# Reordering one decoder-layer kernel: the last tile's eviction, the splits that open a block, and one unit of room in the attention chain

## The chip, the cores and the metric

The kernel runs on one core of a Trainium2 chip. The metric is the device time of one execution in microseconds (us). Before the change the median of three runs is 2895.75 us (2893.29 to 2896.04).

## What is computed

One step of a hybrid decoder layer in fp32, for a prompt of 2048 tokens and a sample group of 8 sequences with 4 tokens each, which share all weights. Cut to what matters:

```python
def hybrid_layer(x, ...):
    u, q, k, v, g_s, g_a = split(x @ w_in)                  # 512, 512, 128, 128, 1024, 1024 columns
    y, state = s5_scan(u, ...)                              # diagonal state space branch
    ya, yb = split(gelu(y) @ w_glu)
    branch_s = ya * sigmoid(yb)
    o = sliding_window_attention(q, k, v, sinks)            # window 128, 8 heads, 2 kv heads
    branch_a = o @ w_attn_br
    merged = sigmoid(g_s) * branch_s + sigmoid(g_a) * branch_a
    x = layer_norm(ALPHA * x + merged @ w_o)                # "x1"
    a, g = split(x @ w_up)                                  # 2 x 2816 columns
    h = gelu(causal_conv3(a)) * g
    return layer_norm(ALPHA * x + h @ w_down)
```

## The kernel before

**Precision.** Every matrix operand is cut into an upper part (fp32r) and a lower part (the rest), and a product is three matmuls: upper with upper, upper with lower, lower with upper. For a weight tile `wr` of 128 x 1024 (a *unit*), ScalarE (ACT in the profile) makes the upper part `wh` and VectorE (DVE) or GpSimd (POOL) the lower part `wl` by a subtraction. `Weights` (lines 181 to 219) does this ahead of the use: `load_to` issues the DMA on SyncE's queue (SP), `split_to(n, eng)` makes the two parts of all units up to `n`. Without `eng`, line 200 gives every third unit's lower part to POOL once 24 units are done; there are four buffers each for `wh` and `wl`, three for `wr`.

**Order.** Each engine's queue holds its instructions in the order in which the Python program issues them. The prompt is done in four blocks of 512 tokens (`body`), and the sample's 32 tokens ride along with block 1. A block goes through its units one after the other: `u` 0 to 3, `k`, `v`, four `q`, eight `gs` and eight `ga` gates (in block 0 the `q` come behind the `gs`), eight `glu`, four `br`, eight `wo`, then 22 pairs `ua`, `ug` and the `dn` units. 512 columns of one unit take TensorE (PE) some 5.5 us.

**Side work.** Between two units the program calls `bg.tick()` (`Background`, lines 48 to 76). Work that was added for this tick is issued then: first all that has no matmuls of its own, then the functions marked `@fills`, whose transposes and small matmuls go into TensorE's queue between two units; within each, what is further along its chain comes first. `ssm_chain` gives a chain of steps s0 to s9 for each quarter of the state space, `attn_chain` (lines 869 to 946) one for each of 4 query blocks x 2 kv heads: a0 scores (PE), a1 row maxima (DVE), a2 exponentials and sums (ACT, DVE), a3 the probabilities `pp` times the reciprocal sums `su` (POOL, 4 instructions), a4_ transposes of `pp` (PE) and their eviction `pt` (ACT), a6 the product with the values (PE), a7 its eviction to `oh` (ACT) and `ol` (DVE). One step is issued each tick. Chain i starts `AS*i//5` ticks behind the first, with 5 in block 0 (`AS0`), 7 in block 1 (`AS1`) and 9 in blocks 2 and 3 (`AS`). In block 0 the first starts at the tick behind the second `ga` unit, so that the last a7 is issued behind `glu` 6.

**Buffers.** PSUM tiles all come from `P()`, a pool of eight banks of 128 x 512; a tile is written only when the last reader of the bank's former tile is done. SBUF work tiles come from `S()`, a pool of 66.

**The stage around x1** (lines 1414 to 1559). The second half of `wo` is done token tile by token tile: `wo_second(t)` gives 24 matmuls, `wo_evict` adds the residual (`xr`, line 1431) and takes the statistics, `ln_scale` makes the reciprocal deviation on POOL (four small instructions, `rs`, lines 1143 to 1146), `ln1` applies it to the two halves of the row, one on ACT, one on DVE (line 1464). `x1_transpose(t)` brings the tile into PSUM by eight PE transposes, and `x1_evict(half)` turns two tiles into the operand of the next layer: `upper` writes the upper parts `x1h` of eight channel groups k, `whole` the exact values `x1f`, `lower` their differences `x1l`. For k below 4 these go through ACT, above through DVE. PE does `wo_second(3)` last, then `first_units` (line 1604): the upper products of the first two up-projection units over tiles 0 and 1, then those with `x1l`, then `x1_transpose(2)` and `x1_transpose(3)`, then unit three, which reads split +3. The order of DVE and POOL between these is written out by hand:

```python
        wo_evict(acc, 2, 1)
        ln_scale(2)
        upper()
        W.split_to(W.pos + 1, V)
        W.split_to(W.pos + 2, G)
        whole()
        ln1(2)
        lower(range(4))
        lower(range(4, 8), G)
        wo_evict(acc3, 3, 1)
        ln_scale(3)
        W.split_to(W.pos + 3, V)
        ln1(3)
        W.split_to(W.pos + 4, G)
```

**The sample's state** (`sample_state_out`, lines 1120 to 1127) is written out behind the last `glu` unit of block 1: for each of two parts a DVE copy `hso`, a PE transpose at once, an ACT eviction, a DMA on POOL's queue.

Of the kernel before, what the change touches and what calls it, by code (L numbers as in the profile page):

```python
# [8 lines left out]
F32 = mybir.dt.float32  # L9
# [3 lines left out]
OP = mybir.AluOpType  # L13
# [66 lines left out]
def tile_hybrid_layer(ctx: ExitStack, tc: tile.TileContext,  # L80
# [5 lines left out]
    V, A, G, T, SP = nc.vector, nc.scalar, nc.gpsimd, nc.tensor, nc.sync  # L86
# [15 lines left out]
    def S(name, cols=512, dt=F32):  # L102
        return pool.tile([128, cols], dt, name=uid(name), tag="s", bufs=SLOTS)
# [7 lines left out]
    def act(out, in_, func=AF.Identity, scale=1.0, bias=0.0, **kw):  # L111
        if func is AF.Identity and not isinstance(bias, bass.AP) and bias == 0.0 and not isinstance(scale, bass.AP):
            A.activation(out, in_, AF.Copy, scale=scale, **kw)  # L113
        else:
            A.activation(out, in_, func, scale=scale, bias=bias, **kw)  # L115
# [4 lines left out]
    def tt(out, a, b, op, eng=V):  # L120
        eng.tensor_tensor(out, a, b, op=op)  # L121
# [46 lines left out]
    order = []  # L168
# [12 lines left out]
    class Weights:  # L181
# [12 lines left out]
        def split_to(self, n, eng=None):  # L194
            while self.splits < min(n, len(order)):
                t = self.raw.pop(self.splits)
                hi = wp.tile([128, 1024], F32R, name=uid("wh"), tag="wh", bufs=4)
                lo = wp.tile([128, 1024], F32R, name=uid("wl"), tag="wl", bufs=4)
                act(hi, t)
                e = eng or (G if self.splits % 3 == 2 and self.splits > 24 else V)  # L200
                tt(lo, t, hi.bitcast(F32), OP.subtract, eng=e)
                self.ready[self.splits] = (hi, lo)
                self.splits += 1
# [17 lines left out]
    W = Weights()  # L221
    bg = Background()
# [60 lines left out]
    def transpose_to(out, in_, k):  # L283
        T.transpose(out, in_, ident[:k, :k])  # L284
# [584 lines left out]
    def attn_chain(B, qb, kv):  # L869
        C = Blk()  # L870
        first = B.b == 0 and qb == 0
        mk = mask[:, 2:4] if first else mask[:, 0:2]
        mk = mk.rearrange("p a k -> p (a k)")

        @fills
        def a0():
            C.s = [P(), P()]
            for j in range(4):
                o = C.s[j // 2][:, (j % 2) * 256:(j % 2) * 256 + 256]
                q = B.q[j][kv][:, qb * 128:(qb + 1) * 128]  # L880
                ks = slice(qb * 128, qb * 128 + 256)
                T.matmul(o, q, kh[kv][:, ks], start=True, stop=False)  # L882
                T.matmul(o, q, kl[kv][:, ks], start=False, stop=True)  # L883

        def a1():
            C.p = [S("pp"), S("pp")]
            C.nm = sm("nm", 4)
            for j in range(4):
                h = 4 * kv + j
                V.tensor_tensor_reduce(out=C.p[j // 2][:, (j % 2) * 256:(j % 2) * 256 + 256],  # L890
                                       in0=C.s[j // 2][:, (j % 2) * 256:(j % 2) * 256 + 256], in1=mk,
                                       scale=-0.125, scalar=nsk[:, h:h + 1], op0=OP.add, op1=OP.min,
                                       accum_out=C.nm[:, j:j + 1])
            C.es = sm("es", 4)
            tt(C.es, C.nm, sk[:, 4 * kv:4 * kv + 4], OP.add)

        def a2():
            C.sum = sm("su", 4)
            for j in range(4):
                o = C.p[j // 2][:, (j % 2) * 256:(j % 2) * 256 + 256]  # L900
                act(o, o, AF.Exp, scale=-1.0, bias=C.nm[:, j:j + 1], accum_out=C.sum[:, j:j + 1])
            act(C.es, C.es, AF.Exp)
            tt(C.sum, C.sum, C.es, OP.add)
            V.reciprocal(C.sum, C.sum)

        def a3():
            for j in range(4):
                o = C.p[j // 2][:, (j % 2) * 256:(j % 2) * 256 + 256]
                ts(o, o, C.sum[:, j:j + 1], eng=G)

        @fills
        def a4_():
            C.t = [P(), P()]
            for kt in range(2):
                for j in range(4):
                    o = (j % 2) * 256 + kt * 128
                    transpose_to(C.t[kt][:, j * 128:(j + 1) * 128], C.p[j // 2][:, o:o + 128], 128)

            B.pt[qb, kv] = [S("pt"), S("pt")]
            for kt in range(2):  # L920
                act(B.pt[qb, kv][kt], C.t[kt])
            C.__dict__.clear()

        @fills
        def a6():
            if kv == 1:
                B.ops[qb] = P()
                for h in range(2):
                    r = slice(64 * h, 64 * h + 64)
                    pt = B.pt.pop((qb, h))  # L930
                    for kt in range(2):
                        T.matmul(B.ops[qb][r, :], vt[:, qb + kt, r], pt[kt], start=(kt == 0), stop=(kt == 1))  # L932

        def a7():
            if kv == 1:
                ps = B.ops.pop(qb)
                sl = slice(qb * 128, (qb + 1) * 128)
                for j in range(4):
                    if j not in B.oh:
                        B.oh[j], B.ol[j] = S("oh", 544, F32R), S("ol", 544, F32R)  # L940
                    act(B.oh[j][:, sl], ps[:, j * 128:(j + 1) * 128])
                for j in range(4):
                    tt(B.ol[j][:, sl], ps[:, j * 128:(j + 1) * 128], B.oh[j][:, sl].bitcast(F32), OP.subtract)
                B.ready += 1

        return [a0, a1, a2, a3, a4_, a6, a7]


    def sample_consts(B):
# [168 lines left out]
        return [c0, None, c1, c2, c4, c6, c8]  # L1118

    def sample_state_out(B):  # L1120
        for r, dst in enumerate((re_s, im_s)):
            t = S("hso")
            V.tensor_copy(t[:, 0:128].rearrange("p (b a) -> p b a", b=8), B.hn[:, r].rearrange("p a b -> p b a"))
            ps = P()
            transpose_to(ps[:, 0:128], t[:, 0:128], 128)
            act(t[:, 128:256], ps[:, 0:128])
            G.dma_start(dst.rearrange("b (a g) p -> (b a) (g p)", g=2), t[:, 128:256])


    def ln_part(B, i, h):  # L1130
# [82 lines left out]
    def body(B, nxt):  # L1213
        n, cols = B.n, B.cols
# [4 lines left out]
        for i in range(4):  # L1219
            hi, lo = (w.rearrange("p (k m) -> p k m", k=2) for w in W.get(("u", i), 0 if B.b else max(0, 3 - i)))  # L1220
            for kk in range(2):
                k = 2 * i + kk
# [39 lines left out]
        ps = full(("k",))  # L1262
        for i, c0, c in segs:
            sl = slice(128 + c0, 128 + c0 + c)
# [3 lines left out]
            for h in range(2):  # L1268
                r = slice(64 * h, 64 * h + 64)
# [8 lines left out]
        ps = full(("v",))  # L1278
# [33 lines left out]
        if B.last:  # L1312
            t = S("kwo")
            ps = P()
# [141 lines left out]
        def ln_scale(i):  # L1456
            scales[i] = ln_stats(B, i)

        def ln1(i):
            m = rows(B, i)  # L1460
            rs = scales.pop(i)
            z = B.z[i]
            act(z[1][:m, 0:512], z[1][:m, 0:512], AF.Identity, scale=rs[:m, 0:1], bias=rs[:m, 1:2])
            ts(z[0][:m, 0:512], z[0][:m, 0:512], rs[:m, 0:1], rs[:m, 1:2], op0=OP.mult, op1=OP.add)
# [22 lines left out]
        def x1_evict(half):  # L1487
            def src(k):
                if half == 2:
                    return tps[4][:, k * 32:(k + 1) * 32]  # L1490
                return tps[half, k // 2][:, (k % 2) * 256:(k % 2) * 256 + 256]

            c0, c = (512, 32) if half == 2 else (half * 256, 256)
            sl = slice(c0, c0 + c)
            f = [S("x1f") for _ in range(4)]
            fk = lambda k: f[k // 2][:, (k % 2) * 256:(k % 2) * 256 + c]

            def affine(out, k):
                if k < 4 or half == 2:
                    act(out, src(k), AF.Identity, scale=g1[:, k:k + 1], bias=b1[:, k:k + 1])  # L1500
                else:
                    ts(out, src(k), g1[:, k:k + 1], b1[:, k:k + 1], op0=OP.mult, op1=OP.add)

            def upper():
                for k in (0, 4, 1, 5, 2, 6, 3, 7):
                    affine(x1h[k][:, sl], k)

            def whole():
                for k in (0, 4, 1, 5, 2, 6, 3, 7):
                    affine(fk(k), k)  # L1510

            def lower(ks=range(8), eng=V):
                for k in ks:
                    tt(x1l[k][:, sl], fk(k), x1h[k][:, sl].bitcast(F32), OP.subtract, eng)
            return upper, whole, lower

        def wo_second(t):
# [23 lines left out]
        ln_scale(2)  # L1541
        upper()
        W.split_to(W.pos + 1, V)
        W.split_to(W.pos + 2, G)
        whole()
        ln1(2)
        lower(range(4))
        lower(range(4, 8), G)
        wo_evict(acc3, 3, 1)
        ln_scale(3)  # L1550
        W.split_to(W.pos + 3, V)
        ln1(3)
        W.split_to(W.pos + 4, G)
        if B.sp:
            for fn in x1_evict(2):
                fn()
# [277 lines left out]
```

## Time and profile before

| | |
|---|---|
| median of 3 runs | 2895.75 us |
| the profiled execution | 2894.74 us |
| its span, first to last instruction | 2892.9 us |
| PE busy | 2833.0 us (98%) |
| PE weight loads | 2415.8 us (84%) |
| DVE, ACT, POOL busy | 59%, 40%, 36% |
| mean granted TensorE clock | 0.992 of 2.4 GHz |

PE is busy nearly all the time, so what can be won by reordering lies in the sixty microseconds in which it is not, and in the stretches in which its clock is granted at half. The share of the other engines says little: a wait ends with the one instruction that PE needs next, wherever that stands in its own engine's queue.

### The profile page before, as it was taken

What the parts mean: (1) busy time and instruction counts of PE and PEld (TensorE: products, weight loads), DVE (VectorE), ACT (ScalarE), POOL (GpSimd) and SP (SyncE); (2) the same over time, 40 slices, a digit from 0 to 9 for tenths busy, and PEclk for the clock granted to TensorE, in tenths of its full rate; (3) what the DMA queues carried; (4) which work ended last, traced back from release to release, by engine and by line L of the source; (5) the groups of instructions that cost most, each with busy time, mean ns of one, the idle gap of its engine ahead of it and who ended that gap; (6) DMA issues with size and microseconds to landing.
All of it is one profiled execution on the core that took longest, in us unless ns stands there. A gap on an engine that the chain in (4) does not pass through costs nothing. (4 is left out here: it accounts for less than half of the span.)

```text
span 2892.9 us, 39211 instructions
## 1 busy us (share of the span) xinstructions
PE 2833.0 (98%) x15168; PEld 2415.8 (84%) x15168; DVE 1696.7 (59%) x2678; ACT 1142.8 (40%) x1991; POOL 1047.3 (36%) x1098
## 2 busy tenths in 40 slices
PE   9989999999999999999999999999999999999998
PEld 8877888888998889989977778888888877888887
DVE  6985676254574467634646645673545854675355
ACT  3335354243335425423424352442343453354241
POOL 1964243111455313512216641351114652252122
PEclk9999999999999999999999999999999999999999
DMA  4422333234532232322326224233244523333232
GB/s 139 150 70 73 124 94 103 92 95 133 165 114 81 74 113 75 91 93 79 117 90 196 81 75 137 73 102 102 88 138 124 166 70 110 102 89 108 88 95 98
DMA packets 415116, 304.30 MB, mean 105 GB/s; under 512 B 52283, under 2 KB 351122, under 8 KB 414914
## 3 DMA queue, kind: packets, MB, share of 16 engines
q1 hardware_dynamic: 412114, 293.84, 33.3%
q0 software_dynamic: 2816, 7.96, 0.8%
q8 instruction: 119, 1.95, 0.3%
q14 instruction: 67, 0.55, 0.1%
HBM read 285.30 MB, written 17.39 MB: 105 GB/s over the span
## 5 line engine op out<-in xcount | busy, mean ns | idle before, releaser
L121 POOL TENSOR_TENSOR wl<-wr,wh 128x1024 fp32r<-128x1024 f32 x144 | 358.6, 2490 | 953.1 <-ACT wh L113 909.8
L113 ACT ACTIVATE wh<-wr 128x1024 fp32r<-128x1024 f32 x448 | 470.5, 1053 | 285.8 <-PE ps L239 187.6
L233 PE MATMUL ps<-x1l,wh 128*128 128x512 f32 (+2 forms) x1856 | 571.8, 343 | 2.0 <-DVE x1l L121 2.0
L233 PE MATMUL ps<-x1h,wh 128*128 128x512 f32 (+2 forms) x1856 | 569.4, 342 | 0.0
L233 PE MATMUL ps<-x1h,wl 128*128 128x512 f32 (+2 forms) x1856 | 568.9, 342 | 0.0
L121 DVE TENSOR_TENSOR wl<-wr,wh 128x1024 fp32r<-128x1024 f32 x304 | 395.5, 1304 | 219.8 <-ACT wh L113 219.2
L233 PEld LDWEIGHTS ps<-x1l,wh 128*128 128x128 f32 x1856 | 327.5, 189 | 45.1 <-DVE x1l L121 2.9
L233 PEld LDWEIGHTS ps<-x1h,wh 128*128 128x128 f32 x1856 | 327.0, 189 | 43.2
L233 PEld LDWEIGHTS ps<-x1h,wl 128*128 128x128 f32 x1856 | 326.4, 189 | 41.2
L233 PE MATMUL ps<-xh,wh 128*128 128x512 f32 (+1 forms) x880 | 288.0, 359 | 7.9 <-DVE q L121 2.5
L233 PE MATMUL ps<-xh,wl 128*128 128x512 f32 (+1 forms) x880 | 282.3, 354 | 1.5 <-DVE wl L121 1.5
L233 PE MATMUL ps<-xl,wh 128*128 128x512 f32 (+1 forms) x880 | 281.8, 353 | 0.0
L118 DVE SCALAR_TENSOR_TENSOR cv<-ae,pc,cv 128x512 f32<-128x512 f32 x176 | 145.6, 827 | 227.0 <-ACT cv L115 223.9
L237 PE MATMUL ps<-wh,hh 128*128 128x512 f32 x704 | 278.7, 396 | 0.0
L239 PE MATMUL ps<-wh,hl 128*128 128x512 f32 x704 | 277.8, 395 | 0.0
L238 PE MATMUL ps<-wl,hh 128*128 128x512 f32 x704 | 277.0, 393 | 0.0
L1571 POOL COPY cc<-ae 128x2 f32<-128x2 f32 x88 | 19.7, 223 | 472.2 <-ACT ae L113 471.3
L233 PEld LDWEIGHTS ps<-xh,wh 128*128 128x128 f32 x880 | 158.0, 191 | 31.8 <-issue 4.4
L233 PEld LDWEIGHTS ps<-xh,wl 128*128 128x128 f32 x880 | 157.4, 190 | 25.7 <-DVE wl L121 2.6
L233 PEld LDWEIGHTS ps<-xl,wh 128*128 128x128 f32 x880 | 157.9, 191 | 20.4
L125 POOL TENSOR_SCALAR pp<-pp,su 128x256 f32<-128x256 f32 x128 | 133.7, 1062 | 70.4 <-ACT pt L113 30.3
L237 PEld LDWEIGHTS ps<-wh,hh 128*128 128x128 f32 x704 | 132.8, 189 | 30.7
(363 smaller groups left out, 4956.9 us busy)
## 6 DMA issues: line engine op xcount, KB each, us to landing
wr<-in_w_up SPq DMA_DIRECT2D x176, 512.0 KB
wr<-in_w_in SPq DMA_DIRECT2D x88, 512.0 KB
wr<-in_w_down SPq DMA_DIRECT2D x88, 512.0 KB
wr<-in_w_glu SPq DMA_DIRECT2D x64, 256.0 KB
wr<-in_w_o SPq DMA_DIRECT2D x32, 512.0 KB
xin<-in_x_prompt SPq DMA_DIRECT2D x32, 256.0 KB
wr<-in_w_in SPq DMA_DIRECT2D x32, 256.0 KB
wr<-in_w_attn_br SPq DMA_DIRECT2D x32, 256.0 KB
```

The lines of the kernel that those rows point to most:

```text
L113: A.activation(out, in_, AF.Copy, scale=scale, **kw)
L118: eng.scalar_tensor_tensor(out, a, s, b, op0=op0, op1=op1, **kw)
L121: eng.tensor_tensor(out, a, b, op=op)
L125: eng.tensor_scalar(out, a, s1, None, op0=op0)
L233: T.matmul(ps[:, :n], w[:, k, :], x[k][:, c0:c0 + n], start=(i == 0), stop=(i == len(ops) - 1))
L237: T.matmul(ps[:m], ah, wh, start=first, stop=False)
L238: T.matmul(ps[:m], ah, wl, start=False, stop=False)
L239: T.matmul(ps[:m], al, wh, start=False, stop=last)
L1571: G.tensor_copy(cc[:, :, f], ae[:, 512:514])
```

## The change

Four edits. The lower parts of a block's four `u` units are never given to POOL by the rule of line 200. An empty step stands ahead of a4_ in the attention chain, so that a4_, a6 and a7 come one tick later. `sample_state_out` makes both copies at once and leaves transposes, eviction and DMAs to a function that comes a tick later among the fills. In the x1 stage `ln1(2)` goes ahead of split +2, the last tile's eviction `wo_evict(acc3, 3, 1)` goes ahead of the lower parts, all eight lower parts are on DVE, `ln1(3)` goes ahead of split +3, split +4 moves from POOL to DVE, and for tiles 0 and 1 six of the eight `whole` parts are on ACT in place of four.

```diff
-                e = eng or (G if self.splits % 3 == 2 and self.splits > 24 else V)
+                e = eng or (G if self.splits % 3 == 2 and self.splits > 24 and order[self.splits][0] != "u" else V)
...
-        return [a0, a1, a2, a3, a4_, a6, a7]
+        return [a0, a1, a2, a3, None, a4_, a6, a7]
...
     def sample_state_out(B):
-        for r, dst in enumerate((re_s, im_s)):
-            t = S("hso")
-            V.tensor_copy(t[:, 0:128].rearrange("p (b a) -> p b a", b=8), B.hn[:, r].rearrange("p a b -> p b a"))
+        t = S("hso")
+        for r in range(2):
+            V.tensor_copy(t[:, r * 128:(r + 1) * 128].rearrange("p (b a) -> p b a", b=8),
+                          B.hn[:, r].rearrange("p a b -> p b a"))
+
+        @fills
+        def rows_out():
             ps = P()
-            transpose_to(ps[:, 0:128], t[:, 0:128], 128)
-            act(t[:, 128:256], ps[:, 0:128])
-            G.dma_start(dst.rearrange("b (a g) p -> (b a) (g p)", g=2), t[:, 128:256])
+            for r in range(2):
+                transpose_to(ps[:, r * 128:(r + 1) * 128], t[:, r * 128:(r + 1) * 128], 128)
+            act(t[:, 256:512], ps[:, 0:256])
+            for r, dst in enumerate((re_s, im_s)):
+                G.dma_start(dst.rearrange("b (a g) p -> (b a) (g p)", g=2), t[:, 256 + r * 128:384 + r * 128])
+        bg.add(1, rows_out)
...
-            def affine(out, k):
-                if k < 4 or half == 2:
+            def affine(out, k, n=4):
+                if k < n or half == 2:
...
             def whole():
-                for k in (0, 4, 1, 5, 2, 6, 3, 7):
-                    affine(fk(k), k)
-
-            def lower(ks=range(8), eng=V):
-                for k in ks:
-                    tt(x1l[k][:, sl], fk(k), x1h[k][:, sl].bitcast(F32), OP.subtract, eng)
+                for k in (0, 6, 1, 2, 7, 3, 4, 5) if half == 0 else (0, 4, 1, 5, 2, 6, 3, 7):
+                    affine(fk(k), k, 4 if half else 6)
+
+            def lower():
+                for k in range(8):
+                    tt(x1l[k][:, sl], fk(k), x1h[k][:, sl].bitcast(F32), OP.subtract)
...
         upper()
         W.split_to(W.pos + 1, V)
+        ln1(2)
         W.split_to(W.pos + 2, G)
         whole()
-        ln1(2)
-        lower(range(4))
-        lower(range(4, 8), G)
         wo_evict(acc3, 3, 1)
         ln_scale(3)
+        lower()
+        ln1(3)
         W.split_to(W.pos + 3, V)
-        ln1(3)
-        W.split_to(W.pos + 4, G)
+        W.split_to(W.pos + 4, V)
```

## Rows read from the trace of the kernel before

**Rows 1.** The page's first part: busy time of each engine over the span

```profile
PE 2833.0 (98%) x15168; PEld 2415.8 (84%) x15168; DVE 1696.7 (59%) x2678; ACT 1142.8 (40%) x1991; POOL 1047.3 (36%) x1098
```

**Rows 2.** PE's waits: line, what released it, total us, times, longest us

```profile
PE ps L284 <- DVE xr L127: 7.5, 4, 1.9
PE ps L284 <- POOL pp L125: 6.3, 8, 2.2
...
PE ps L238 <- POOL wl L121: 5.5, 1, 5.5
...
PE ps L233 <- DVE nm L890: 3.6, 3, 1.7
...
PE ps L284 <- DVE hso L1123: 2.2, 1, 2.2
...
PE ps L233 <- ACT y L113: 1.5, 1, 1.5
```

**Rows 3.** Four stretches: us, busy (x instructions) by engine, granted clock, DMA, GB/s

```profile
1104.20:1107.50 3.30, 3.30 (x17) 3.30 (x17) 0.00 (x0) 3.30 (x12) 2.23 (x1) 0.50 0.27 81
363.70:367.10 3.40, 3.40 (x30) 3.40 (x31) 2.52 (x6) 3.40 (x8) 2.19 (x1) 1.00 0.33 100
...
1534.30:1537.60 3.30, 3.01 (x7) 2.47 (x8) 0.00 (x0) 0.00 (x0) 3.20 (x5) 0.50 0.53 152
1636.70:1643.40 6.70, 5.92 (x21) 5.05 (x22) 1.24 (x1) 2.14 (x3) 4.81 (x6) 0.50 0.01 4
```

**Rows 4.** Timeline of PE, block 3's x1 stage: start, us, instruction, [idle before]

```profile
2510.14 0.39 PE L239 MATMUL ps<-wh,mgl 128*128 128x512 f32 x1
...
2515.22 1.79 PE L233 MATMUL ps<-x1l,wh 128*128 128x256 f32 x13 [0.49 <-DVE x1l L121]
...
2519.79 1.17 PE L284 MATMUL ps<-ident,xr 128*128 128x128 f32 x8 [1.90 <-DVE xr L127]
```

**Rows 5.** Timeline of DVE in the same stage

```profile
2510.78 0.88 DVE L127 TENSOR_SCALAR xr<-xr,rs 128x512 f32<-128x512 f32 x1
2511.58 3.59 DVE L121 TENSOR_TENSOR x1l<-x1f,x1h 128x256 fp32r<-128x256 f32 x4
2515.09 0.67 DVE L118 SCALAR_TENSOR_TENSOR xr<-xr,ps 128x512 f32<-128x512 f32 x1
...
2516.65 1.18 DVE L121 TENSOR_TENSOR wl<-wr,wh 128x1024 fp32r<-128x1024 f32 x1
2519.18 0.55 DVE L127 TENSOR_SCALAR xr<-xr,rs 128x512 f32<-128x512 f32 x1 [1.35 <-POOL rs L1146]
...
2524.33 2.76 DVE L121 TENSOR_TENSOR x1l<-x1f,x1h 128x256 fp32r<-128x256 f32 x8
```

**Rows 6.** Timeline of POOL in the same stage

```profile
2508.97 2.41 POOL L121 TENSOR_TENSOR wl<-wr,wh 128x1024 fp32r<-128x1024 f32 x1 [1.63 <-ACT wh L113]
2511.32 3.56 POOL L121 TENSOR_TENSOR x1l<-x1f,x1h 128x256 fp32r<-128x256 f32 x4
2516.83 1.08 POOL L1143 TENSOR_SCALAR rs<-mv 128x1 f32<-128x1 f32 x1 [1.94 <-DVE mv L1142]
```

**Rows 7.** Timeline of ACT at the start of block 2

```profile
1519.96 1.04 ACT L113 ACTIVATE wh<-wr 128x1024 fp32r<-128x1024 f32 x1
```

**Rows 8.** Timeline of DVE at the start of block 2

```profile
1526.23 0.69 DVE L121 TENSOR_TENSOR xr<-xr,g2t 128x512 f32<-128x512 f32 x1 [2.92 <-ACT xr L115]
```

**Rows 9.** Timeline of PE at the start of block 2

```profile
1534.59 0.82 PE L238 MATMUL ps<-wl,xh 128*128 128x512 f32 x1 [5.48 <-POOL wl L121]
```

**Rows 10.** Timeline of POOL in block 2's gates

```profile
1633.91 7.60 POOL L125 TENSOR_SCALAR pp<-pp,su 128x256 f32<-128x256 f32 x8
```

**Rows 11.** Timeline of DVE at the end of block 0's glu units

```profile
282.46 0.88 DVE L121 TENSOR_TENSOR ol<-ps,oh 128x128 fp32r<-128x128 f32 x4
...
287.43 0.69 DVE L118 SCALAR_TENSOR_TENSOR gs<-gs,tb 128x512 f32<-128x512 f32 x1
```

**Rows 12.** Timeline of PE at the start of block 0's br units

```profile
286.11 0.40 PE L233 MATMUL ps<-ol,wh 128*128 128x512 f32 x1
```

## The prediction

> **What bounds the kernel.** I read the page's busy times first: TensorE (PE) is busy for 2833.0 us, 98% of the span [rows 1]. So DVE, ACT and POOL matter only where PE waits for one of their instructions; I read PE's waits next. Six lines of that list hold 26.6 us of them [rows 2]: the last token tile's normalised row (7.5 us, once in each block), the probabilities (6.3), one weight split on POOL (5.5), PSUM banks that a row maximum or a state-space eviction still reads (3.6 and 1.5), the sample's state copy (2.2). Third, the granted clock. After most of these waits it is 0.50, TensorE's level of 1.2 GHz: in the 3.3 us after the row wait of block 1, in those after the split wait, in 6.7 us after the probabilities of block 2 [rows 3]. Four more of 3.3 us or so follow waits of this list: in blocks 2 and 3 after the row wait, in block 3 after the probabilities, and after the state copy; three stand elsewhere. After block 0's row wait, as long as the others, the clock stayed at 1.00 [rows 3]. A wait therefore costs its length and, mostly, half of a 3.3 us stretch behind it, 1.65 us. For probabilities, split and state the change takes away what PE waits for; the question is what is late next.
>
> **Part 1, the x1 stage, four times.** I work it in block 3. PE's last accumulation for tile 3 starts at 2510.14 and is done by 2510.5, but its eviction starts on DVE at 2515.09 [rows 4, 5], behind a normalisation of 0.88 and four lower parts of 0.90 each; POOL's four take 0.89 each beside them [rows 5, 6]. Alone on DVE, eight lower parts take 2.76, 0.35 each [rows 5]. Today DVE has done split +1 and four whole parts by 2510.78 [rows 5]; in the new order it has done split +1, the normalisation of tile 2 and two whole parts by about then, and takes the eviction at once: 1.56 from its start to the next instruction [rows 5], so 2512.4. Eight lower parts then end at 2515.2, just when the last of the mixed set ends now. The deviation on POOL starts at 2512.6 rather than 2516.83; from that start to DVE's use it takes 2.35 now [rows 5, 6], so it is ready at 2515.0. DVE's normalisation of tile 3 (0.55) ends near 2515.8 in place of 2519.7. PE's products with x1l end at 2517.0 [rows 4]; tile 2's transposes take 1 us more. Tile 3 is there two microseconds before PE wants it. The wait goes in each block, 7.5 us. The 0.49 for x1l [rows 4] stays about as it is. Late next is split +3: ACT makes its upper part behind tile 3's row, so DVE's part (1.18) ends near 2518.3, against a first use near 2519. Split +4 on DVE in place of POOL (2.41, [rows 6]) has 3 us more. Behind them DVE's eight lower parts of tiles 2 and 3 end near 2526, PE wants the first near 2526.4: covered by half a microsecond. Three half-clock stretches go with the waits, 3 x 1.65 = 5.0. Part 1: **12.5 us**. Bounds: if the lower parts take 0.90 each though POOL has none, 7.2 in all, the last ends at 2519.6, tile 3's transposes start near 2521.4, 1.6 later than now [rows 4], and nothing is won but 6.4 us lost; above, the four x1l waits go too, 2.0 more. I take 2.76, since that row is the same set of eight on the same engine.
>
> Here a rule speaks against the change. The rows show the pair of engines taking 0.9 for what DVE alone does in 0.35. The Trainium skill (SBUF — State Buffer, "Who interferes with whom") says that a VectorE instruction with two SBUF inputs and a GpSimd instruction that reads SBUF exclude each other for the whole instruction, whichever issues first. By that rule POOL's split +2, if it starts just ahead of the lower parts, holds all eight back by its full length, and the first rival below would be the forecast.
>
> **Part 2, a block's first splits.** The wait of 5.48 in block 2 is for POOL's lower part of unit u3: its upper part was ready at 1521.0 [rows 7], PE wanted it at 1529.1 [rows 9]. DVE sits idle for 2.92 us until 1526.23 in this gap [rows 8]; the split costs it 1.18 alone [rows 5], 2.4 if it takes as long as on POOL [rows 6], and is done by 1526 in either case. So 5.5 + 1.65 = **7.1 us**. The other three `u` units moved (one more in block 2, one each in blocks 1 and 3) cost PE no wait today and are made a unit or more ahead: nothing, or 2.4 each if that cover fails.
>
> **Part 3, one unit of room.** In block 2 POOL multiplies two chains' probabilities from 1633.91 on, eight in 7.60 [rows 10]; the first four, for which PE waits, are done at 1637.7. One tick later PE has first done the other chain's transposes, scores, a gate unit (5.5) and a state-space step: some 4 us of cover. The same holds in block 3. The 6.3 us of rows 2 go, and of the half-clock stretches 6.7 and 3.3 us, worth 3.35 and 1.65: 11.3. Against it, the last eviction of a chain also comes a tick later. In blocks 1 to 3 there is room behind it; in block 0 it falls between the last `glu` unit and `br`, which reads `oh` and `ol`. Today PE goes on with its first `ol` product at 286.11 [rows 12]. With the change `ol` stands on DVE behind the last gate product, which ends at 288.1 [rows 11]; its first of four pieces takes 0.88 / 4. PE waits until 288.35, **2.2 us lost**, plus 0 to 1.65 of clock (half: 0.8). Lastly, banks are taken in the order of their release (my reading of the three waits that follow). With a4_ moved, PE's waits of 1.48 and 1.14 in block 0 and 1.65 in block 1 (in the nm and y lines of [rows 2]) meet other, free banks, but two units in block 1, `ga` 5 and `glu` 0, meet banks whose maxima are taken just then: 0.4 and 1.9 by the same DVE instructions' times. Block 0 gains 2.2 of 2.6, since ACT is nearly full there; block 1 loses 0.7, and 0.5 of clock. Part 3: 11.3 - 3.0 + 2.2 - 1.2 = **9.3 us**; bounds 5 and 14.
>
> **Part 4, the state copy.** PE goes straight on to `br`, whose inputs are long there: 2.2 + 1.65 = **3.9 us**. Transposes, eviction and two DMAs come two units later; POOL's queue holds nothing between that PE needs sooner, since the split behind them waits for a later ACT instruction.
>
> **The sum.** 12.5 + 7.1 + 9.3 + 3.9 = 32.8. The profiled execution took 2894.74, which gives 2861.9; the median of the runs is 1.0 above it, so **2863 us**.
>
> **Rivals.** *POOL in the way* (the skill's rule, at its worst): split +2 starts as the lower parts do, they end 2.4 later, 2517.8, PE's x1l products then end near 2519, tile 3's transposes start near 2520, and part 1 is worth nothing. For it: ACT has one more row ahead of split +2's upper part, so POOL starts near 2509.8 in place of 2508.97 [rows 6]. Against: even so it ends at 2512.2, before the lower parts start. 2863 + 12.5 = 2875.5. *The clock stays low*: waits go, but other short idle times in the same places (0.49 for x1l, the new ones in blocks 0 and 1) keep the half-clock stretches, 5.0 + 1.65 + 5.0 + 1.65 = 13.3: 2876. Against: gaps of 1.65 and 1.48 have no such stretch behind them. *The time comes back*: PE is earlier by 33 us, but DVE and ACT, which set row maxima and gates, are not, and new waits take most of it: no change, 2892. For it: block 0, where ACT leaves little; against: block 3 has no split wait and shows no wait after its first units. *Slower, at SP's queue*: `pp` keeps its pair of the 66 work tiles one unit longer; if the pool is full, state-space table loads on SP wait for a tile, and all weight loads behind them. One such delay is a unit, 5.5 us; six that reach PE undo the gain, eight give 2863 + 44 = 2907. For it: 24 groups of such loads in blocks 1 to 3. Against: nothing in PE's list waits for a weight load.
>
> **Chances.** Forecast 0.62 (2856 to 2870), POOL in the way 0.14, clock 0.10, time comes back 0.09, SP 0.05. Two runs of this kernel tell 0.2% apart, 5.8 us. Faster 0.91, the same 0.06, slower 0.03. The range 2856 to 2877 takes the first three, with 2 us for x1l and 5 for part 3 below.
>
> **What would show it.** DVE's statistics of tile 3 ahead of eight lower parts of 0.35; no PE wait for xr, pp, wl of `u`, hso; one new wait of about 2 us for `ol` at 286; granted clock near 0.997. Wrong if lower parts stay at 0.9, if PE waits for split +3 or +4, or if the row maxima's waits grow.

## The result and the profile after

The changed kernel takes 2864.62 us (median of 4 runs, 2863.94 to 2864.77) against 2895.89 in the same measurement: ratio 0.9895, 95% interval 0.9882 to 0.9907. The forecast was 2863. The profiled execution took 2864.77, its span is 2862.9.

The page's first part, kernel after [rows 1]:

```profile
PE 2822.4 (99%) x15168; PEld 2408.5 (84%) x15168; DVE 1695.7 (59%) x2694; ACT 1146.0 (40%) x1998; POOL 1015.5 (35%) x1074
```

PE's waits, kernel after (line, what released it, total us, times, longest), those of its lines against [rows 2] that bear on the four edits:

```profile
PE ps L284 <- DVE nm L890: 1.8, 1, 1.8
PE ps L233 <- DVE nm L890: 1.8, 3, 0.9
PE ps L233 <- POOL wl L121: 1.8, 1, 1.8
...
PE ps L233 <- DVE ol L121: 1.0, 1, 1.0
...
PE ps L233 <- ACT oh L113: 0.9, 1, 0.9
```

The lines for xr, pp, hso and the u unit's wl are gone, and so is that for x1l (2.0 us, 4 times in the kernel before), which the forecast had left in place. New are `oh` and `ol` (1.9 together, forecast as 2.2), a bank that a row maximum still reads (the first line), and a wait for a split on POOL, at another place than before.

The x1 stage of block 3, the timelines of PE, DVE and POOL in the kernel after (start, us, instruction, idle before), against [rows 4 to 6]:

```profile
2487.95 2.12 PE L233 MATMUL ps<-x1l,wh 128*128 128x256 f32 x16
2489.90 1.91 PE L284 MATMUL ps<-ident,xr 128*128 128x128 f32 x16
```

```profile
2484.38 0.69 DVE L118 SCALAR_TENSOR_TENSOR xr<-xr,ps 128x512 f32<-128x512 f32 x1 [0.44 <-PE ps L239]
2485.10 0.69 DVE L1141 BATCH_NORM_STATS2 st<-xr 128x6 f32<-128x512 f32 x1
2485.83 0.21 DVE L1149 BATCH_NORM_AGGREGATE mv<-st 128x2 f32<-128x12 f32 x1
2485.96 2.72 DVE L121 TENSOR_TENSOR x1l<-x1f,x1h 128x256 fp32r<-128x256 f32 x8
2488.59 0.54 DVE L127 TENSOR_SCALAR xr<-xr,rs 128x512 f32<-128x512 f32 x1
```

```profile
2483.05 2.41 POOL L121 TENSOR_TENSOR wl<-wr,wh 128x1024 fp32r<-128x1024 f32 x1 [1.92 <-ACT wh L113]
```

DVE now waits 0.44 us for PE's last product and evicts tile 3 at once; the eight lower parts take 2.72; the sixteen transposes of tiles 2 and 3 are one row without a wait. POOL's split +2 ends at 2485.46, half a microsecond ahead of the first lower part; so it does in the other three blocks.

The granted clock in three stretches (us, busy by engine, clock, DMA), kernel after:

```profile
289.00:292.30 3.30, 3.30 (x8) 2.65 (x9) 0.50 (x3) 0.00 (x0) 0.00 (x0) 0.50 0.00 0
1088.00:1103.00 15.00, 15.00 (x120) 14.53 (x119) 12.02 (x30) 12.91 (x32) 4.08 (x6) 1.00 0.48 141
1541.70:1545.00 3.30, 3.30 (x10) 2.56 (x9) 1.65 (x2) 0.00 (x0) 3.21 (x3) 0.50 0.92 244
```

The second is block 1's whole x1 stage: no half clock. The first and the third stand behind the new waits, for `ol` and for the split.

The new wait for a split, PE's and POOL's timelines in block 2, kernel after:

```profile
1541.02 0.50 PE L233 MATMUL ps<-xh,wl 128*128 128x512 f32 x1 [1.78 <-POOL wl L121]
```

```profile
1535.09 1.30 POOL L121 TENSOR_TENSOR xr<-xr,g2t 128x512 f32<-128x512 f32 x1
1536.47 2.17 POOL L121 TENSOR_TENSOR xr<-xr,b2t 128x512 f32<-128x512 f32 x1
1538.61 2.35 POOL L121 TENSOR_TENSOR wl<-wr,wh 128x1024 fp32r<-128x1024 f32 x1
```

It is the block's first q unit, the next that line 200 gives to POOL; ahead of it stand the output rows of the block before.

**Where the time came from.** The same matmul, by its count from the first, starts so much earlier or later in the changed kernel than in the kernel before; the difference over a stage is what the stage gave. The second column is the prediction, the third the kernel after, the last the kernel that has only this part (below). All by one profiled execution of each kernel, in us:

```
stage                      forecast   after   part alone
x1, blocks 0, 1, 2, 3       -12.5     -15.8     -16.0    (after: 2.8, 4.1, 4.5, 4.4)
u split, block 2             -7.1      -3.5      -5.0    (after: -7.1, then +3.6)
empty step, block 0          +0.8      +2.7      +1.2
            block 1          +1.2      -1.4      -1.4
            block 2          -7.5      -8.1      -8.1
            block 3          -3.8      -3.5      -3.6
state copy                   -3.9      -3.8      -4.0
everything else               0        +3.3
at PE's end                 -32.8     -30.1
```

In the last line but one are 1.1 us at the start (PE's first wait, for its input, is 5.2 in this execution and 3.8 in the one before) and 1.2 given back little by little between the x1 stage of block 1 and the next block.

These are single executions, and they hold the half-clock stretches that each of them happened to have: of the 15.8 of the x1 stage some 11.4 are PE's waits and the rest is half clock. The medians below give another split: the four parts alone are worth 10.3, 8.6, 10.5 and 1.7 us, 31.1 together, against 31.3 for the whole change. So the parts add up as far as medians tell; how much is the x1 stage's and how much the u split's is known to some microseconds only.

### The profile page after: what moved, and what is told of

It is laid out like the page before. It is cut to its first block, busy times and chain, and to the rows that moved or that the text cites. A ratio compares the mean times of both kernels' runs of the same rounds, so it can differ in the third digit from the quotient of the medians.

```text
span 2862.9 us, 39202 instructions
## 1 busy us (share of the span) xinstructions
PE 2822.4 (99%) x15168; PEld 2408.5 (84%) x15168; DVE 1695.7 (59%) x2694; ACT 1146.0 (40%) x1998; POOL 1015.5 (35%) x1074
## 4 chain that ended last, share of the span: by engine, by line
PE 66%; POOL 1%; DVE 1%; ACT 0%; issue 0%; POOLq 0%; DVEq 0%; ACTq 0%
PE ps L233 43%; PE ps L237 6%; PE ps L239 6%; PE ps L238 6%; PE ps L284 2%; PE ps L932 1%; PE ps L742 0%; PE ps L245 0%; PE ps L247 0%; PE ps L882 0%; PE ps L883 0%; PE ps L801 0%; PE ps L802 0%; PE ps L800 0%; DVE xr L121 0%
## 5 line engine op out<-in xcount | busy, mean ns | idle before, releaser
L121 POOL TENSOR_TENSOR wl<-wr,wh 128x1024 fp32r<-128x1024 f32 x136 | 338.5, 2489 | 905.0 <-ACT wh L113 889.0
L121 DVE TENSOR_TENSOR wl<-wr,wh 128x1024 fp32r<-128x1024 f32 x312 | 406.2, 1306 | 214.8 <-ACT wh L113 213.7
L239 PEld LDWEIGHTS ps<-wh,hl 128*128 128x128 f32 x704 | 132.2, 188 | 30.8
```

The costliest lines, as they stand in the source:

```text
L239: T.matmul(ps[:m], al, wh, start=False, stop=last)
```

## The experiments

**Each part alone.** Four kernels, each the kernel before with one of the four edits.

> The kernel before with the x1 stage's new order alone. The prediction's part 1: no wait for xr in any of the four blocks, three half-clock stretches fewer, 12.5 us less than the kernel before, near 2883; 2 more if the waits for x1l go as they did in the kernel after. The waits for the probabilities, the split of u3 (5.5) and the state copy stay as they were. Rival (the time comes back: an earlier PE meets row maxima and gates that are no earlier): the waits of the later stages grow by what the stage gave, 2893 to 2895.

Measured: 2883.91 (median of 5) against 2894.25, ratio 0.9966 (0.9952 to 0.9980), so 10 us. The waits for x1l went too, and those of the other parts stayed as they were, in the waits of PE:

```profile
PE ps L284 <- POOL pp L125: 6.1, 7, 2.3
...
PE ps L238 <- POOL wl L121: 5.5, 1, 5.5
...
PE ps L284 <- DVE hso L1123: 2.2, 1, 2.2
```

The stage gave 16.0 in the trace, whose execution (2879.10, mean granted clock 0.994) was the fastest of the five; the other four have 0.992 or 0.993 and 2883.8 to 2884.7. Hardly any of it came back behind the stage. The medians give this part 10 us (5.8 to 13.9 by the interval), less than the trace's 16.0; where the other four executions spent the difference isn't shown, since only the fastest was profiled.

> The kernel before with the u units' lower parts on VectorE alone. The prediction's part 2: the wait of 5.48 and its half-clock stretch go, 7.1 us less, 2888.7. Second theory, from the trace of after: POOL is still busy with the output rows of the block before when the next split that falls to it, that of block 2's first q unit, stands in its queue; PE waits for that one instead, some 1.8 us with a half-clock stretch behind it, so that only 7.1 - 1.8 - 1.65 = 3.7 us are won, near 2892.

Measured: 2885.69 (7 runs), ratio 0.9969 (0.9958 to 0.9980), 8.6 us. The second theory's wait is there. PE's and POOL's timelines in block 2, this kernel:

```profile
1551.91 0.50 PE L233 MATMUL ps<-xh,wl 128*128 128x512 f32 x1 [1.88 <-POOL wl L121]
```

```profile
1547.37 2.17 POOL L121 TENSOR_TENSOR xr<-xr,b2t 128x512 f32<-128x512 f32 x1
1549.51 2.35 POOL L121 TENSOR_TENSOR wl<-wr,wh 128x1024 fp32r<-128x1024 f32 x1
```

The first q unit's lower part stands on POOL behind the output rows of the block before and ends at 1551.86. PE gains 7.1 us at u3, as forecast, and gives 2.1 back here. No half clock followed this wait (it did in the kernel after), and the three stretches behind the row waits of blocks 1 to 3 were missing as well, while two others stood at 769 and 793 us. The waits are as the second theory said, the clock is not. Why the median is better than its 2892 isn't shown: the profiled execution (2887.73) is the slowest of the seven.

> The kernel before with the empty step ahead of the probabilities' transposes alone. The prediction's part 3: the 6.3 us of waits for pp and the half-clock stretches behind them go, a wait of about 2 us for oh and ol opens at the start of block 0's br units: 9.3 us less, 2886.5. Rival (the row maxima are what holds the chain, and the free unit only moves the wait): waits for nm or pp of the same sum stand elsewhere, 2894 or more.

Measured: 2883.75, ratio 0.9963 (0.9950 to 0.9975). A second run of the same kernel gave the trace that is read here:

> The kernel before with the empty step alone, again, for a profile. By the prediction's part 3: no wait for pp (6.3), two new ones of 0.9 and 1.0 for oh and ol in block 0, one of 1.8 there in place of 1.48 and 1.14, in block 1 0.4 and 0.6 in place of 1.65: PE's waits fall by 6.8 us, 3 to 5 of half clock with them; median near 2884. Rival: waits for pp or nm of as many us elsewhere.

Measured: 2883.61 (5 runs) against 2894.07, ratio 0.9963 (0.9950 to 0.9975), 10.5 us. PE's waits, this kernel:

```profile
PE ps L284 <- DVE nm L890: 1.9, 1, 1.9
PE ps L233 <- DVE nm L890: 1.8, 3, 0.8
...
PE ps L233 <- DVE ol L121: 1.0, 1, 1.0
...
PE ps L233 <- ACT oh L113: 0.9, 1, 0.9
```

No wait for pp is left in the list, and the new ones are those of the kernel after: they belong to the empty step.

> The kernel before with the sample's state written out a unit later alone. The prediction's part 4: the wait of 2.2 us for hso and the half-clock stretch behind it go, 3.9 us less, 2892. Rival: PE meets another late operand at the start of br and waits there as long, 2895.

Measured: 2892.51 (10 runs), ratio 0.9993 (0.9984 to 1.0003): 1.7 us, between 0.9 lost and 4.6 won, so neither nothing nor the forecast 3.9 is excluded. At its place the part gave 4.0, but little of that reached the end. In this execution 1.2 had been lost ahead of it, in block 0, and 1.4 went behind the split of u3, where half clock lasted 6.8 us in place of 3.4 (the wait itself is 5.4, as before). And in block 1's x1 stage, where this execution had no half clock behind the row's wait, nothing was won: PE ran ahead and met the lower parts of tiles 2 and 3. PE's and DVE's timelines there, this kernel:

```profile
1111.01 2.74 PE L233 MATMUL ps<-x1l,wh 128*128 128x288 f32 x8 [0.50 <-DVE x1l L121]
```

```profile
1110.54 2.76 DVE L121 TENSOR_TENSOR x1l<-x1f,x1h 128x256 fp32r<-128x256 f32 x8
```

Eight such products take 1.22 us where nothing holds them (those with wl just ahead); here they take 2.74, at DVE's pace of one lower part each 0.34.

**Inside the x1 stage: which of its edits is needed.** Three kernels, each the kernel after with one edit of the stage undone or worsened. The six `whole` parts on ACT, the earlier `ln1(2)` and `ln1(3)` and split +4 on DVE were not taken back one by one; what each of these is worth isn't shown. In the first kernel `lower` gets its two arguments back:

```diff
-        lower()
+        lower(range(4))
+        lower(range(4, 8), G)
```

> The kernel after, with four of tile 0 and 1's eight lower parts on POOL again, the eviction still ahead of them. Theory that the eight on DVE are needed: POOL starts its four behind the deviation, at about 2487.8 in block 3, and ends them some 3.6 us later, 2491.3; PE wants the last at 2488.9 and waits some 2.4 us for x1l in each block, 9.6 us and up to 6.6 of half clock: 2874 to 2881. Rival, that the place of the eviction alone does it: no wait above 0.5, 2865 to 2867.

Measured: 2880.82 against 2893.74, ratio 0.9956 (0.9941 to 0.9971): by the medians 16 us slower than the kernel after. PE's waits, and POOL's timeline in block 3:

```profile
PE ps L233 <- POOL x1l L121: 8.3, 12, 1.3
```

```profile
2501.37 3.97 POOL L121 TENSOR_TENSOR x1l<-x1f,x1h 128x256 fp32r<-128x256 f32 x4
```

The eight on DVE are needed; the place of the eviction alone isn't enough.

```diff
-        wo_evict(acc3, 3, 1)
-        ln_scale(3)
         lower()
+        wo_evict(acc3, 3, 1)
+        ln_scale(3)
```

> The kernel after, with tile 3's eviction and deviation behind the eight lower parts again, all eight still on DVE. Theory that the order is what counts: tile 3's row comes 1.9 us late in each block, 7.5 us and up to 5 of half clock, 2872 to 2877. Rival, that eight lower parts of 0.35 on DVE alone make room enough in either order: they end near 2486.8 in block 3, the eviction at 2488.3, the deviation at 2490.1, tile 3's row on DVE at 2490.7 against a use at 2490.9: no wait above 0.3, 2865 to 2867.

Measured: 2874.19, ratio 0.9936 (0.9919 to 0.9953), 9.6 us slower than after: the order counts too. My rival, in which either order would do, missed one thing. DVE's and POOL's timelines in block 3, the first with a window that ends with the first lower part, then PE's waits:

```profile
2490.50 1.88 DVE L121 TENSOR_TENSOR x1l<-x1f,x1h 128x256 fp32r<-128x256 f32 x1
```

```profile
2489.69 2.41 POOL L121 TENSOR_TENSOR wl<-wr,wh 128x1024 fp32r<-128x1024 f32 x1 [1.92 <-ACT wh L113]
```

```profile
PE ps L233 <- DVE wl L121: 4.5, 6, 0.9
...
PE ps L284 <- DVE xr L127: 3.7, 4, 0.9
```

The first lower part takes 1.88 us and ends 0.28 after POOL's split +2 (2492.10); the other seven take 0.41 (0.34 apart). So the eight take 4.23, not 2.7, and tile 3's row and then split +3 come late, 0.9 and 0.76 us in each block. With the eviction ahead, DVE does that (0.69, against 0.67 in [rows 5], where POOL does nothing) while POOL makes its split, and starts the lower parts when POOL is done.

```diff
         ln1(2)
-        W.split_to(W.pos + 2, G)
         whole()
+        W.split_to(W.pos + 2, G)
```

> The kernel after, with split +2 issued behind the whole parts, so that POOL makes it while DVE makes the lower parts: the first rival of the prediction set up on purpose. ACT makes its upper part till 2485.9 in block 3, POOL runs from there 2.4 us, to 2488.3; DVE's lower parts start at 2486.0. If the two exclude each other for a whole instruction: DVE's first lower part shows 2.4 us more (2.7), the eight end near 2491.0, PE waits some 2.1 us for x1l in each block, 8 us and up to 6.6 of clock, 2873 to 2880. If they share access by access, as 0.90 against 0.35 would also allow: two or three parts of 0.9, the rest 0.35, end near 2490.2, waits of 1.2, 2869 to 2875. If POOL is not in the way: 2865.

Measured: 2873.13, ratio 0.9928 (0.9912 to 0.9945), 8.5 us slower than after. DVE's timeline in block 3 up to the first lower part, all eight by their tile (ns: least, median, longest), and POOL's timeline:

```profile
2491.04 2.50 DVE L121 TENSOR_TENSOR x1l<-x1f,x1h 128x256 fp32r<-128x256 f32 x1
```

```profile
L121 DVE TENSOR_TENSOR x1l<-x1f,x1h x8: 411/412/2495, 2491.0 to 2495.5; 128x256 fp32r<-128x256 f32 x8
```

```profile
2490.89 2.37 POOL L121 TENSOR_TENSOR wl<-wr,wh 128x1024 fp32r<-128x1024 f32 x1 [4.64 <-ACT wh L113]
```

One lower part is held for POOL's whole instruction (until 2493.26) and the seven behind it run at 0.41. By its duration that is the first of the three outcomes expected, and it is so in all four blocks (2.44 to 2.50); sharing access by access would have given two or three parts of 0.9. The Trainium skill (SBUF — State Buffer, "Who interferes with whom") says so of a VectorE instruction with two SBUF inputs against GpSimd reading SBUF; the trace agrees, with 2.50 and 1.88 against 0.41. The price came out somewhat otherwise than expected: PE waited 1.04 in each block for the late split itself, which my sum had not looked at, and some 0.8 on the lower parts, about 2 us together.

**The clock.** The kernel before once more, unchanged:

> The kernel before once more, for a second profiled execution. If a half-clock stretch belongs to the wait ahead of it: the same seven stretches behind the rows, the split, the probabilities and the state copy, and none behind block 0's row. If it belongs to the execution (a wait of 1.9 us may or may not bring one): the same waits within 0.1 us, other stretches behind them, and a span that goes with their sum, half of it.

Measured: 2896.88, one run. Its waits are those of [rows 2] within 0.1 us. The half clock stood behind the same waits of this kernel as before, in the x1 stages of blocks 1 to 3 and not in block 0 (3.3 us from the end of each row's wait, blocks 0 and 1):

```profile
364.10:367.40 3.30, 3.30 (x29) 3.30 (x30) 2.40 (x6) 3.30 (x8) 2.07 (x1) 1.00 0.35 99
1106.40:1109.70 3.30, 3.30 (x17) 3.30 (x16) 0.04 (x1) 3.30 (x11) 2.40 (x2) 0.50 0.26 79
```

One more stretch of 3.4 us stands at 792 and one of 6.8 in place of 3.4 behind the split. But in the kernels with the u splits alone or the state copy alone, where the same waits of 1.9 us in blocks 1 to 3 come 1 to 6 us earlier or later in the execution, none is followed by it, and with the empty step alone one of the three (block 2's) is; block 1, u splits alone:

```profile
1107.60:1110.90 3.30, 3.30 (x29) 3.30 (x30) 0.00 (x0) 3.30 (x11) 2.06 (x1) 1.00 0.36 109
```

So neither theory holds whole: the same kernel repeats most of its stretches, and another kernel with the same waits, a few us earlier or later, may have one or none. What decides it stays open. A stretch that is gone can't be credited to the edit alone; the wait can.

**A better version.** The new waits of the kernel after, taken away:

```diff
-        return [a0, a1, a2, a3, None, a4_, a6, a7]
+        return [a0, a1, a2, a3] + ([None] if B.b else []) + [a4_, a6, a7]
-                ... and order[self.splits][0] != "u" else V)
+                ... and order[self.splits][0] not in "ukvq" else V)
```

> The kernel after with two edits: the empty step in blocks 1 to 3 alone, and the lower parts of k, v and q units on DVE like those of u. If the new waits of the kernel after have the causes that its trace names: in block 0 the waits for oh and ol (0.86 and 0.98, and 1.65 of half clock) and the new one of 1.85 go and those of 1.48 and 1.14 come back, 2.7 us less; in block 2 the wait of 1.78 for POOL's split and its half clock go, 3.4 us less: 2864.6 - 6.1 = 2858.5. Rival, that a wait taken away there shows up one unit on: 2863 to 2865.

Measured: 2857.43, ratio 0.9875 (0.9861 to 0.9890). Again, beside the kernel after:

> The kernel after once more, beside the others of this call: 2864 to 2865 if chips agree. Its new waits for oh, ol and the q unit's split again within 0.1 us; the half-clock stretches behind them as in the run before if they belong to the wait, otherwise not.

> The kernel after with the empty step in blocks 1 to 3 alone and the k, v and q units' lower parts on DVE, again, beside the kernel after: 7 us less than that, if the first look was right; 6.1 by the sum made for it; within 2 us of it if the two looks differed by the chip.

Measured: kernel after 2864.35 (ratio 0.9897, 0.9882 to 0.9912; its new waits within 0.1 us, half clock again behind those for `ol` and the split), this one 2858.17 (0.9875, 0.9862 to 0.9889): 6.2 us less, 6.1 by the sum. PE's waits, this kernel: those for `oh`, `ol` and POOL's wl are gone and the two of block 0 are back:

```profile
PE ps L233 <- DVE nm L890: 2.9, 4, 1.1
PE ps L233 <- ACT y L113: 1.5, 1, 1.5
```

## Why the prediction came out right, point by point

**The total** is 1.6 us off. By the traces two terms missed by more than 3 us in opposite directions and cancelled, so that it came out this near is partly luck. By the medians of the parts alone (10.3, 8.6, 10.5, 1.7 against 12.5, 7.1, 9.3, 3.9) the misses are 1.2 to 2.2 us each, and every forecast lies in its part's interval.

**Part 1 (12.5; measured 15.8).** The order, the 2.76, the deviation and splits +3 and +4 came as worked out; "tile 3 is there two microseconds before PE wants it" holds. The step that failed is "The 0.49 for x1l [rows 4] stays about as it is". I compared the end of the set of eight with the end of the mixed set. PE takes the lower parts one by one in the order of k, and DVE now makes them in that order, each 0.34 behind the last; before, k = 3 was the last of DVE's four. Part k was there before product k. That is the 2.0 which the prediction had put in its upper bound. The other 1.3 come from reading a wait's cost off the list, which counts idle time from the listed end of the product before. The profile lists a product as ending after the next one has started (products of 0.28 us start 0.12 apart here), so by starts a wait costs more. PE's timelines in block 0, where no half clock follows, in the kernel before and with the x1 stage alone:

```profile
358.01 0.61 PE L233 MATMUL ps<-x1l,wh 128*128 128x256 f32 x3
359.11 1.80 PE L233 MATMUL ps<-x1l,wh 128*128 128x256 f32 x13 [0.49 <-DVE x1l L121]
360.75 1.03 PE L284 MATMUL ps<-ident,xr 128*128 128x128 f32 x8
363.67 1.09 PE L284 MATMUL ps<-ident,xr 128*128 128x128 f32 x8 [1.89 <-DVE xr L127]
```

```profile
358.17 2.14 PE L233 MATMUL ps<-x1l,wh 128*128 128x256 f32 x16
360.15 1.91 PE L284 MATMUL ps<-ident,xr 128*128 128x128 f32 x16
```

From the first product with x1l to tile 2's transposes it is 2.74 us before and 1.98 alone: 0.76 for a listed 0.49. By the starts of the single transposes the row's wait costs 2.05 for a listed 1.89. The four blocks give 11.4 us of waits for a listed 9.5; the three half-clock stretches gave 4.9, of which 0.4 were lost again right behind.

**Part 2 (7.1; measured 3.5).** The size at u3 was right to the tenth. The step that failed is what I left out behind it: the other three u units "cost PE no wait today", and the next split on POOL behind them wasn't looked at. POOL's timeline at the same place in the kernel before, from the first deviation to that split:

```profile
1517.02 0.22 POOL L1143 TENSOR_SCALAR rs<-mv 128x1 f32<-128x1 f32 x1 [15.04 <-DVE mv L1142]
...
1523.19 0.22 POOL L1143 TENSOR_SCALAR rs<-mv 128x1 f32<-128x1 f32 x1 [0.75 <-DVE mv L1142]
...
1544.60 1.63 POOL L121 TENSOR_TENSOR xr<-xr,b2t 128x512 f32<-128x512 f32 x1
1546.19 2.84 POOL L121 TENSOR_TENSOR wl<-wr,wh 128x1024 fp32r<-128x1024 f32 x1
```

From the first to the end of the last POOL takes 32 us, with u3's split (2.3) among them, and 31 in the kernel after without it. Of the 2.3 some 1.6 came back in POOL's other instructions. The last output row takes 2.17 (above) in place of 1.63, and a step of the second deviation stands beside u3's split, which is now on DVE, until that is done (in the kernel with the u splits alone, too). POOL's and DVE's timelines, kernel after:

```profile
1515.90 1.29 POOL L1150 TENSOR_SCALAR rs<-mv 128x1 f32<-128x1 f32 x1 [0.76 <-DVE mv L1149]
```

```profile
1515.95 1.16 DVE L121 TENSOR_TENSOR wl<-wr,wh 128x1024 fp32r<-128x1024 f32 x1
```

PE's way to that unit is 7 us shorter, so the split, done at 1540.96, was needed at 1539.24. It cost 1.8 and, in this execution, as much again at half clock. With it on DVE both went (the better version).

**Part 3 (9.3; measured 10.3).** The waits for pp went, with their clock: 11.6 of the 11.3. `oh` and `ol` cost 1.84 against 2.2, but as two waits: ACT's eviction to `oh` stood behind the last gate's tanh, too, which I had not followed. The reading of the banks was half right: the old three waits went and `ga` 5 waits the 0.40 foretold, but `glu` 0 waits 0.58, not 1.9, and the transposes of `pp` themselves met a bank under a row maximum in block 0 (1.85), which I hadn't seen. So block 1 won 1.4 rather than lose 1.2 and block 0 lost 2.7 rather than 0.8.

**Part 4 (3.9; measured 3.8)** as worked out, by the trace. Alone its median is 1.7 better, with an interval that holds both nothing and 3.9; in its one trace 1.4 went to the longer half clock behind the u3 split, which the kernel before shows in its second execution too.

**The rivals.** *POOL in the way*: the mechanism is real (2.50 for one part; by the prediction's own 2515.2 and 2.41 the lower parts would end at 2517.6, not 2517.8), but its condition is not met by the change: POOL's split is done 0.5 us before the lower parts start. *The clock stays low*: no, the kernel after has five stretches against ten, and two of the five stand behind its own new waits. *The time comes back*: in part, 3.6 at the q unit. *SP's queue*: nothing in PE's waits is for a weight load.

## What to carry to other kernels

When a wait goes, follow every engine's queue to its next instruction that PE needs: by PE's time it is later by what was won, and the queue that held PE is the first to look at. Where two engines share a set of small two-input SBUF instructions, try the whole set on the faster one, and put work with a PSUM input beside the other engine's long SBUF instruction. Judge a part by its waits in the trace and by kernels with it alone, not by the half-clock stretches of one execution.

## What the runs showed that was not expected

Half clock after a wait of 1.9 us came in three of four blocks in two executions of the kernel before, in none in two kernels whose waits are equally long, and in one block in a third. Where it did not come, 1.6 us were not always won: with the state copy alone, PE stood for the lower parts instead in block 1. Of eight lower parts beside POOL's split, not several ran slower: one stood still until the split was done. The same holds the other way round: a POOL step of 0.22 us took 1.29 beside DVE's split.
